# A transformer trunk step in float32 on one core: the first unit and the last output without Strassen sums, start in a written order, pooling rows by pairs

## The chip, the cores and the metric

The kernel runs on one core of a Trainium2 chip. Five engines work side by side, each through its own instructions in order: PE (TensorE, matmuls; its weight loads are shown apart as PEld), DVE (VectorE), ACT (ScalarE), POOL (GpSimd) and SP (SyncE), which here only issues DMAs. PE writes its results to PSUM, eight banks of 128x512 float32 (`banks`); everything else lies in SBUF or, as `dram` tiles, in the chip's memory. The metric is device time of one execution in microseconds (us).

## The reference

One inference step of a hybrid trunk with one layer of each kind, on 512 prompt frames and 8 x 16 sample frames (640 rows in all), in float32. Cut to what matters here:

```python
h = rmsnorm(x, norm_a[l])
z = h @ w_in_a[l]                          # 2048 -> 2 x 4096
u, gate = z[..., :E_A], z[..., E_A:]
y, st = pool_mix(u, pool_prev[l], pos0, w_grp_a[l], scale_a[l])   # trailing means of 2, 4, 8, 16 frames, then a map in each of 4 groups
x = x + (y * jax.nn.silu(gate)) @ w_out_a[l]
new_pool.append(st)                        # last 15 rows of u
...
hk = rmsnorm(x, norm_kv)
kvf = hk @ w_kv
```

After it come keys, values, forget gates, attention over a cache of 256 rows, an output projection and a last norm. All ten outputs are computed.

## The kernel before

**Precision.** Every float32 operand is split in two parts of the faster type float32r: `hi` is a rounded copy made by ACT, `lo` is the rest, a subtraction on DVE. A product is three matmuls: wh x hi, wh x lo, wl x hi. The activations lie transposed: 128 channels by 640 frames, as two halves of 320 (`HALF`).

**Units.** The projection to `u` and the gate is cut into 32 units of 256 output columns; 16 are of kind u, 16 of kind g, in the order u00, u01, g00, u02, g01 and so on. A unit multiplies a 2x2 block of weights with a 2x2 block of activations by Strassen's scheme: seven products m1 to m7 instead of eight, on sums of blocks (`OPER` says which). Eight `Side`s hold the activations, 256 channels each: four blocks, of which three (`bh`, `bl`) serve as they are and four sums of blocks (`th`, `tl`) are made by `blocks_t`. Weights come in slabs of 512 channels (four a unit): `fetch` loads one into `raw` (three buffers), `prep` makes its sums on DVE and splits raw and sums. `pair8` runs a unit, 4 slabs x 7 products x 2 sides x 3 = 168 matmuls, and calls `tick` twice in each slab, by which small jobs (`pool_rows`, `residual`) put an instruction or two into PE's order. `combine` puts the seven products together on DVE.

**Start.** The five row tiles are loaded, normalised (squares on ACT with a running sum, `newton_rsqrt`, scaling on DVE), transposed on PE and copied to the sides. The first unit goes through `first_unit`: all four weight slabs are held at once (the fourth in a pool of its own), and the products on plain blocks run ahead of those on sums.

**A u unit** also transposes 120 old rows (`st`), makes the pooled difference `dd` with shifted additions on POOL (`sw`, one to four of them), stores it, and copies the last 15 rows of each sample stream to `us`. `pool_rows` transposes the two halves of `us` to bank 7 one after the other, with a copy `po` to SBUF and a store on POOL's queue after each.

**Groups.** For each of four groups `y_pair` makes four tiles of y (96 plain matmuls each), times the gate, split as sides 4 to 7; then `out_pair` makes eight pairs of output tiles, 84 Strassen matmuls each, and adds them to the stream in memory (`xacc`) with accumulating DMAs on POOL's queue. In the last group the sum has to be read back: the first part of an output is added in memory, the stream is loaded as `x1` (L589), three more products are added to it on DVE (L605), and the result is stored to `xres`, squared (`squares`, summed by POOL, L640) and split (`split_x`) for the next projections. Tiles 8 to 15 are split after the loop, since their places are in use until then.

**The rest** opens new pools (`wp` for weights, `big`) in the memory that the first part frees, and starts with `prime` and `proj`: weights loaded at L716, scaled by the norm's gain on DVE (L722), split at L730 and L732, multiplied at L701.

**Order.** PE's instructions stand in the order of the program. The other engines' order is made by a scheduler that follows estimated times; a pool's address is set by the order in which pools are opened, and a tile waits for the tiles that held its memory before.

Of the kernel before, what the change touches and what calls it, by code (L numbers as in the profile page):

```python
# [39 lines left out]
def tile_yoco_step(ctx, tc, i, o):  # L40
# [36 lines left out]
    ident = const.tile([P, P], F32, name="ident")  # L77
    make_identity(nc, ident)
    inv = const.tile([P, 16], F32, name="inv")
    for t in range(16):  # L80
        nc.vector.memset(inv[:, t : t + 1], 1.0 / (t + 1))
# [42 lines left out]
    OPER = {"m1": (0, 0), "m6": (5, 5), "m5": (4, 3), "m7": (3, 4), "m2": (2, 2), "m3": (6, 1), "m4": (1, 6)}  # L124
# [12 lines left out]
    xb_, wa, misc = pool(sa, "xb"), pool(sa, "wa"), pool(sa, "misc")  # L137
# [27 lines left out]
    def blocks_t(sd, x4, t, eng=None):  # L165
        eng = eng or nc.vector
        eng.tensor_tensor(t[:, 0, :], x4[:, 0, :], x4[:, 1, :], op=ALU.subtract)
        eng.tensor_tensor(t[:, 1, :], x4[:, 2, :], x4[:, 0, :], op=ALU.add)
        eng.tensor_tensor(t[:, 2, :], x4[:, 2, :], t[:, 0, :], op=ALU.add)
        eng.tensor_tensor(t[:, 3, :], x4[:, 3, :], t[:, 2, :], op=ALU.subtract)  # L170
        sd.th, sd.tl = (tslot(sd.j, q, [P, 4, HALF], F32R) for q in "hl")
        nc.scalar.activation(sd.th, t, AF.Copy)  # L172
        nc.vector.tensor_tensor(sd.tl, t, sd.th.bitcast(F32), op=ALU.subtract)  # L173
# [17 lines left out]
    fourth = []  # L191

    def wbufs(n, shape):

        j = 3 if n == 3 else n % 3 if n < NA else (2, 0, 3, 1)[(n - NA) % 4]
        if j < 3:
            two = [wa.tile(shape, F32R, tag=f"w{q}{j}", name=f"w{q}") for q in "hl"]
            return two, [[t[:, k : k + 1] for k in range(2)] for t in two]
        if n == 3:
            two = [fourth[0].tile(shape, F32R, tag=f"w{q}", name=f"w{q}") for q in "hl"]  # L200
            return two, [[t[:, k : k + 1] for k in range(2)] for t in two]
        return None, [[bslot(k, q, [shape[0], 1] + shape[2:], F32R) for k in range(2)] for q in "hl"]

    def prep():
        n = nprep[0]
        raw = loaded.pop(n).rearrange("p (a b) (s n) -> p a (b s) n", a=2, n=P)
        if loads[n][0] == "s":
# [3 lines left out]
            eng = nc.gpsimd if n >= len(loads) - 16 else nc.vector  # L211
            eng.tensor_tensor(sums[:, :, 2, :], sums[:, :, 1, :], raw[:, :, 1, :], op=ALU.add)
            eng.tensor_tensor(sums[:, :, 3, :], raw[:, :, 3, :], sums[:, :, 2, :], op=ALU.subtract)  # L213
# [56 lines left out]
    cvue = [misc.tile([P, HALF], F32, tag=f"c{q}", name=f"c{q}") for q in "vue"]  # L270
# [26 lines left out]
    for kind, g, p in units:  # L297
        c0 = (E_A if kind == "g" else 0) + g * G_A + p * 2 * P
        for s in range(4):
            loads.append(("s", win[:, 4 * s : 4 * s + 4, c0 : c0 + 2 * P]))  # L300
    for g in range(4):
# [4 lines left out]
        for c in range(8):  # L306
            for s in range(2):
                loads.append(("s", wout[:, g * 8 + 4 * s : g * 8 + 4 * s + 4, c * 2 * P : (c + 1) * 2 * P]))
# [4 lines left out]
    fourth.append(p0)  # L313
# [4 lines left out]
    gains = [bslot(6 + q // 2, "hl"[q % 2], [P, 512]) for q in range(4)]  # L318
    x4s = [tslot(4 + j // 2, "hl"[j % 2], [P, 4, HALF]) for j in range(8)]
    small = pool(start, "small")  # L320

    idle = small.tile([P, P], F32, name="idle")
    nc.vector.memset(idle, 0.0)
    for _ in range(8):
        nc.tensor.matmul(banks[:, 7, :P], idle, idle, start=True, stop=True)
# [4 lines left out]
    def half_rows(t):  # L330
# [4 lines left out]
    half_rows(0)  # L335
    for q in range(4):
        dma(gains[q], i["norm_a"][0][q * 512 : (q + 1) * 512].partition_broadcast(P))
    half_rows(1)
    fetch()
    half_rows(2)  # L340
    half_rows(3)
    half_rows(4)
    for _ in range(2):
        fetch()
    ssq = small.tile([P, TT, 4], F32, name="ssq")
    nbank = [0]
    for t in range(TT):
        ts = slice(t * P, (t + 1) * P)
        n = D // len(rows[t])
        for q in range(4):  # L350
            c = q * 512 % n
            nc.scalar.activation(banks[:, 7, :], rows[t][q * 512 // n][:, c : c + 512], AF.Square, accum_out=ssq[:, t, q : q + 1])
        v = small.tile([P, 1], F32, tag="v", name="v", bufs=2)
        nc.vector.tensor_reduce(v, ssq[:, t, :], axis=AX.X, op=ALU.add)
        nc.vector.tensor_scalar(v, v, 1.0 / D, EPS, op0=ALU.mult, op1=ALU.add)
        rs = small.tile([P, 1], F32, tag="rs", name="rs", bufs=2)
        newton_rsqrt(small, v, rs, [P, 1], "nr")
        for q in range(4):
# [954 lines left out]
```

## Time and profile before

| what | value |
|---|---|
| time, median of 3 runs (lowest, highest) | 2930.67 us (2927.9, 2931.53) |
| the profiled execution | 2930.98 us, span 2929.3 us |
| mean granted clock of PE | 0.981 |
| PE, DVE, ACT, POOL busy | 2794.5, 1935.2, 1027.0, 390.5 us |
| DMA | 390.36 MB, mean 133 GB/s |

The span is from the first to the last instruction. Busy times are unions over an engine's instructions. "Clock" is the share of full clock that PE was granted. A wait is given to what ended it, as far as the semaphores show. A row of the timeline gives start, duration, engine, line, operation, output and input names with their shapes, and in brackets the idle time ahead of it with what ended it. A row of a group gives count, busy time, mean duration in ns, and idle time ahead with what ended it.

```profile
## 2 busy tenths in 40 slices
PE   5899999999999999999986999999999999999998
PEld 4799999989999999999985999999999999999887
DVE  7777877787777848586674755655656666656434
ACT  6333333333334434343332232333333333334222
POOL 1312223133240110202244000000000000000000
PEclk9799999999999999999997999999999999999999
```

Each digit is a fortieth of the span, 73 us. PE falls below nine tenths in the first two and around the twentieth; its clock falls in the second and about the twentieth too.

### The profile page before, as it was taken

To read this page: it belongs to the slowest core of one execution; us is meant where nothing else is said; L and a number is where in the kernel's file an instruction comes from. 1 tells how busy PE (TensorE), PEld (TensorE's weight loads), DVE (VectorE), ACT (ScalarE), POOL (GpSimd) and SP (SyncE) were. 2 spreads that over 40 slices of the span, in tenths; PEclk is the share of its full clock that TensorE was granted. 3 is DMA by queue.
4 is the path that set the end of the run, shared out by engine and by line. 5 is a ranking of instruction groups with operands and counts; after the bars stand their busy time and mean duration, and the time that the engine had idled before them with its cause. 6 is when DMAs were issued, how large, how long until landed. Compare 5 with 4: busy or idle time off the path is not lost.

```text
span 2929.3 us, 46530 instructions
## 1 busy us (share of the span) xinstructions
PE 2794.5 (95%) x18410; PEld 2691.4 (92%) x18410; DVE 1935.2 (66%) x3350; ACT 1027.0 (35%) x1720; POOL 390.5 (13%) x426
## 2 busy tenths in 40 slices
PE   5899999999999999999986999999999999999998
PEld 4799999989999999999985999999999999999887
DVE  7777877787777848586674755655656666656434
ACT  6333333333334434343332232333333333334222
POOL 1312223133240110202244000000000000000000
PEclk9799999999999999999997999999999999999999
DMA  4344443433435786868466644455544455554823
GB/s 136 98 126 130 132 128 121 134 110 115 131 107 182 182 166 171 170 169 171 121 178 175 163 120 118 115 121 124 131 119 115 119 121 119 120 121 105 148 84 111
DMA packets 677643, 390.36 MB, mean 133 GB/s; under 512 B 323920, under 2 KB 632704, under 8 KB 677296
## 3 DMA queue, kind: packets, MB, share of 16 engines
q1 hardware_dynamic: 652256, 320.61, 41.3%
q0 software_dynamic: 25168, 66.78, 10.4%
q8 instruction: 144, 2.36, 0.3%
q14 instruction: 75, 0.61, 0.1%
HBM read 299.34 MB, written 87.95 MB: 132 GB/s over the span
## 4 chain that ended last, share of the span: by engine, by line
PE 42%; DMA 4%; DVE 1%; SPq 1%; POOL 1%; issue 1%; ACT 0%; DVEq 0%; POOLq 0%; ACTq 0%
PE banks L701 30%; PE banks L1205 5%; PE banks L1133 2%; DMA xacc<-m 2%; PE banks L1034 1%; DMA xt<-xres 1%; PE banks L110 1%; SPq L1243 1%; DMA x<-xacc 1%; POOL bh L640 1%; PE banks L1044 0%; PE banks L1045 0%; PE banks L1046 0%; DVE yn L1246 0%; PE banks L1146 0%
## 5 line engine op out<-in xcount | busy, mean ns | idle before, releaser
L246 PE MATMUL banks<-th,wh 128*128 128x320 f32 x1408 | 447.9, 318 | 12.6 <-ACT th L172 12.2
L246 PE MATMUL banks<-tl,wh 128*128 128x320 f32 x1408 | 442.9, 315 | 17.7 <-DVE tl L173 17.7
L246 PE MATMUL banks<-th,wl 128*128 128x320 f32 x1408 | 441.3, 313 | 0.0
L701 PE MATMUL banks<-th,whi 128*128 128x320 f32 x2048 | 399.6, 317 | 22.7 <-ACT whi L730 22.7
L701 PE MATMUL banks<-tl,whi 128*128 128x320 f32 x2048 | 384.0, 309 | 0.0
L246 PE MATMUL banks<-bh,wh 128*128 128x320 f32 x1056 | 332.8, 315 | 14.8 <-DVE x L605 9.8
L701 PEld LDWEIGHTS banks<-th,whi 128*128 128x128 f32 x2048 | 316.1, 189 | 29.0 <-ACT whi L730 23.0
L246 PE MATMUL banks<-bl,wh 128*128 128x320 f32 x1056 | 331.8, 314 | 3.1 <-DVE bl L163 3.1
L246 PE MATMUL banks<-bh,wl 128*128 128x320 f32 x1056 | 331.6, 314 | 0.6 <-DVE wl L89 0.6
L732 DVE TENSOR_TENSOR wlo<-raw,whi 128x512 fp32r<-128x512 f32 x272 | 186.3, 686 | 212.9 <-ACT whi L730 209.9
L701 PEld LDWEIGHTS banks<-tl,whi 128*128 128x128 f32 x2048 | 321.9, 188 | 0.0
L730 ACT ACTIVATE whi<-raw 128x512 fp32r<-128x512 f32 x272 | 171.7, 632 | 398.6 <-PE banks L701 234.3
L89 DVE TENSOR_TENSOR wl<-raw,wh 128x768 fp32r<-128x768 f32 (+1 forms) x200 | 209.4, 1048 | 142.5 <-ACT wh L86 136.3
L86 ACT ACTIVATE wh<-raw 128x768 fp32r<-128x768 f32 (+1 forms) x200 | 173.5, 869 | 342.8 <-issue 156.0
L246 PEld LDWEIGHTS banks<-tl,wh 128*128 128x128 f32 x1408 | 270.4, 192 | 20.9 <-DVE tl L173 20.9
L246 PEld LDWEIGHTS banks<-th,wh 128*128 128x128 f32 x1408 | 270.5, 192 | 17.2 <-ACT th L172 15.2
L246 PEld LDWEIGHTS banks<-th,wl 128*128 128x128 f32 x1408 | 270.0, 192 | 0.0
L89 DVE TENSOR_TENSOR wl<-sums,wh 128x1024 fp32r<-128x1024 f32 x176 | 223.6, 1271 | 42.5 <-ACT wh L86 41.9
L86 ACT ACTIVATE wh<-sums 128x1024 fp32r<-128x1024 f32 x176 | 185.2, 1052 | 188.6 <-DVE sums L213 183.4
L701 PE MATMUL banks<-th,wlo 128*128 128x320 f32 x1024 | 233.7, 309 | 0.2 <-DVE wlo L732 0.2
L701 PE MATMUL banks<-tl,wlo 128*128 128x320 f32 x1024 | 233.7, 309 | 0.0
L246 PEld LDWEIGHTS banks<-bh,wh 128*128 128x128 f32 x1056 | 203.3, 193 | 16.4 <-DVE x L605 10.3
(376 smaller groups left out, 5156.1 us busy)
## 6 DMA issues: line engine op xcount, KB each, us to landing
raw<-in_w_in_a SPq DMA_DIRECT2D x128, 512.0 KB, 4.0
raw<-in_w_out_a SPq DMA_DIRECT2D x64, 512.0 KB, 4.9
raw<-in_w_kv SPq DMA_DIRECT2D x128, 256.0 KB, 3.1
raw<-in_w_in_b SPq DMA_DIRECT2D x128, 256.0 KB, 3.0
raw<-in_w_grp_a SPq DMA_DIRECT2D x32, 512.0 KB, 5.6
kc<-in_cache_k SPq DMA_DIRECT2D x64, 256.0 KB, 4.1
vc<-in_cache_v SPq DMA_DIRECT2D x16, 1024.0 KB, 7.4
raw<-in_w_out_b SPq DMA_DIRECT2D x64, 256.0 KB, 3.2
```

Source lines behind the costliest of these rows:

```text
L86: a = nc.scalar.activation(hi, x, AF.Copy)
L89: nc.vector.tensor_tensor(lo, x, hi.bitcast(F32), op=ALU.subtract)
L110: nc.tensor.transpose(out, x, ident[:n, :n])
L246: nc.tensor.matmul(bank[:, :HALF], w[kk][:, a, :], x, start=first and q == 0, stop=last and q == 2)
L640: nc.gpsimd.tensor_tensor(sqs[0], sqs[0], s, op=ALU.add)
L701: nc.tensor.matmul(acc_[:, s, :HALF], w, x[:, s * HALF : (s + 1) * HALF], start=f, stop=l)
L730: nc.scalar.activation(hi, raw, AF.Copy)
L732: nc.vector.tensor_tensor(lo, raw, hi.bitcast(F32), op=ALU.subtract)
L1034: nc.tensor.matmul(sp[rows, b % 2 * PAST : (b % 2 + 1) * PAST], qs[:, rows], kct[:, b * PAST : (b + 1) * PAST], start=True, stop=True)
L1133: nc.tensor.matmul(po[32 * q : 32 * q + 32, :P], pts[:, j, 32 * q : 32 * q + 32], vc[:, 4 * q + j, :], start=(j == 0), stop=False)
L1205: nc.tensor.matmul(out, (ol if q == 2 else oh)[k][:, ts], wl if q == 1 else wh, start=first and q == 0, stop=last and q == 2)
L1243: dma(xt[at].rearrange("p t (j r) -> p t j r", r=32), xres[n * 512 : (n + 1) * 512].rearrange("(j c) (t a r) -> a c t j r", c=32, a=4, r=3 ...
```

## The change

1. **Start.** DVE, ACT and POOL follow the program's order until the eight sides stand. The sample's rows go first (tile 4, then 0 to 3). The gains are read as one row each and spread over 128 partitions by a matmul with ones into banks 0 to 3. Squares go 1024 columns at a time into SBUF, four idle matmuls (`busy(4)`) follow each tile.
2. **First unit without sums.** Its four slabs are of kind "p" (no sums); `plain_slab` runs all eight block products, 192 matmuls, into banks 0 to 3. The first block of each side gets a split of its own (`b12`). The sums of the sides are made in place (`sums_t`), five on DVE and three on POOL, and split behind the plain slabs' work. The unit's results are copied by ACT instead of `combine`. The fourth weight buffer is gone.
3. **Pooling rows by pairs.** Both halves of `us` lie in one tile, copied by POOL instead of ACT, transposed one after the other into one bank, copied once, stored once, on SP's queue. `st`, `us`, `po` share a ring of two buffers.
4. **Output, first pair of groups 0 to 2** (`c == 0`): all seven products on sides 0 to 2 first, then those on side 3.
5. **Last group.** y is split plain (`yk`), weights are of kind "p", and `last_pair` makes an output pair with 96 plain matmuls. `load_stream_pair` loads the stream's sum ahead of its pair; the result goes back to `xacc` (on SP's queue) and `xres` is gone. The squares' sum is stored by SP.
6. **Pools.** `wa` is opened ahead of `xb`, so that `wp` later lies where the weights were.

The core of the diff:

```diff
-    xb_, wa, misc = pool(sa, "xb"), pool(sa, "wa"), pool(sa, "misc")
+    wa, xb_, misc = pool(sa, "wa"), pool(sa, "xb"), pool(sa, "misc")
...
+    def sums_t(x4, t=None, eng=None):
+
+        eng, t = eng or nc.vector, x4 if t is None else t
+        eng.tensor_tensor(t[:, 1, :], x4[:, 0, :], x4[:, 1, :], op=ALU.subtract)
+        eng.tensor_tensor(t[:, 0, :], x4[:, 2, :], x4[:, 0, :], op=ALU.add)
+        eng.tensor_tensor(t[:, 2, :], x4[:, 2, :], t[:, 1, :], op=ALU.add)
         eng.tensor_tensor(t[:, 3, :], x4[:, 3, :], t[:, 2, :], op=ALU.subtract)
...
-            loads.append(("s", win[:, 4 * s : 4 * s + 4, c0 : c0 + 2 * P]))
+            loads.append(("s" if loads[3:] else "p", win[:, 4 * s : 4 * s + 4, c0 : c0 + 2 * P]))
...
+    steady.enter_context(tc.manual_schedule(engines={mybir.EngineType.DVE, mybir.EngineType.Activation, mybir.EngineType.Pool}))
...
+    def plain_slab(s):
+        wh, wl = parts.pop(0)
+        for j in (2 * s, 2 * s + 1):
+            hi = [b12[j][:, 0, :]] + [xs_[j].hi(q) for q in range(3)]
+            lo = [b12[j][:, 1, :]] + [xs_[j].lo(q) for q in range(3)]
+            for k in range(2):
+                for n in range(2):
+                    for q, (w, x) in enumerate(((wh, hi), (wh, lo), (wl, hi))):
+                        for h in range(2):
+                            nc.tensor.matmul(first[2 * n + h], w[j % 2][:, 2 * k + n, :], x[2 * k + h],
+                                             start=j + k + q == 0, stop=j == 7 and k == 1 and q == 2)
+        done()
...
+    blocks(6)
+    blocks(7)
+    sums(7)
+    sums(0)
+    sums(1)
+    split_t(xs_[0], x4s[0])
+    fetch()
+    prep()
+    split_t(xs_[1], x4s[1])
+    sums(2)
+    plain_slab(3)
...
+        yield
+        tq = tbank()
         for b in range(2):
-            yield
-            tq = tbank()
-            transpose(tq[: NB * PAD, :P], uss[b])
-            po = pu.tile([NB * PAD, P], F32, tag="po", name="po")
-            nc.scalar.activation(po, tq[: NB * PAD, :P], AF.Copy)
-            store2(o["pool_sample"][0].rearrange("b s e -> (b s) e")[:, c0 + b * P : c0 + (b + 1) * P], po)
+            transpose(tq[: NB * PAD, b * P : (b + 1) * P], uss[b])
+        po = pu.tile([NB * PAD, 2 * P], F32, tag="po", name="po", bufs=2)
+        nc.scalar.activation(po, tq[: NB * PAD, : 2 * P], AF.Copy)
+        store(o["pool_sample"][0].rearrange("b s e -> (b s) e")[:, c0 : c0 + 2 * P], po)
...
+        if c == 0:
+
+            for s, kks in ((0, (0, 1)), (1, (0,))):
+                for m in ORDER:
+                    go(m, s, kks)
+            for m in ORDER[:4]:
+                go(m, 1, (1,))
...
+    def last_pair(c, x1, yk):
+        pp = plain(yk)
+        for b in range(2):
+            a = halves(x1[b])
+            for s in range(2):
+                nc.vector.tensor_tensor(a[:, s, :], a[:, s, :], pp[b][s], op=ALU.add)
+            k = 2 * c + b
+            dma(xacc[c][b * P : (b + 1) * P, :], x1[b])
+            squares(k, x1[b])
+            if k < 8:
+                split_x(k, x1[b])
+            else:
+                late.append((k, x1[b]))
```

How it moves instructions is seen at three places. A name with a number is one tile. The first place is DVE ahead of the second unit. Before, `th_159`, `tl_166` and `bh_494` hold blocks of a side and their rounded copies, `x4_498` the sums of such blocks, `tl_504` the low part of a side's sums; `raw`, `sums`, `wh` and `wl` belong to weight slabs:

```order
L163 TENSOR_TENSOR bl_495<-tl_166,bh_494 128x960
L213 TENSOR_TENSOR sums_474<-raw_446,sums_474 128x2x128
L167 TENSOR_TENSOR x4_498<-th_159 128x320
L169 TENSOR_TENSOR x4_498<-th_159,x4_498 128x320
L170 TENSOR_TENSOR x4_498<-th_159,x4_498 128x320
L89 TENSOR_TENSOR wl_479<-sums_474,wh_478 128x2x512
L209 TENSOR_TENSOR sums_714<-raw_484 128x2x256
L173 TENSOR_TENSOR tl_504<-x4_498,th_503 128x1280
L173 TENSOR_TENSOR tl_513<-th_507,th_512 128x1280
```

Now, `th_132` and `tl_133` hold the sums of a side in place, `tl_732` and `tl_736` their low parts, `raw_659` to `wl_744` are the fifth slab, the first of the second unit, and `dd_802` is the pooled difference of the first unit, which needs POOL's `sw_800`:

```order
L84 TENSOR_TENSOR tl_732<-th_132,th_731 128x1280
L84 TENSOR_TENSOR tl_736<-tl_133,th_735 128x1280
L201 TENSOR_TENSOR sums_739<-raw_659 128x2x256
L203 TENSOR_TENSOR sums_739<-sums_739,raw_659 128x2x128
L548 TENSOR_TENSOR dd_802<-sw_800,inv_179 128x1
L550 SCALAR_TENSOR_TENSOR dd_802<-sw_800,ub_783 128x511
L204 TENSOR_TENSOR sums_739<-raw_659,sums_739 128x2x128
L84 TENSOR_TENSOR wl_744<-raw_659,wh_743 128x2x384
```

Before, a slab's sums (`sums_474`) stood between the sides' blocks and sums. Now the sums of the sides come right ahead of the fifth slab, and the rest of that slab (L204, L84) stands behind `dd_802`.

The second place is SP, which issues most DMAs, at the end of the last group. Before, `bh_14915` and `bl_14916` are loads of the stream (`xacc3`), `sqd` is the sum of squares on its way back to SBUF, `raw` from `in_w_kv` the first weights of the next projection, and the rest are inputs of later stages:

```order
L589 DMA bh_14915<-xacc3_90 128x640
L589 DMA bl_14916<-xacc3_90 128x640
L1018 DMA kc_15487<-in_cache_k 32x64x32
L1157 DMA wr_15259<-in_w_kv 128x16x16
L858 DMA bf_15288<-in_b_f 128x16
L873 DMA cl_15303<-in_cache_logf 128x8x16 x2
L780 DMA sq2_15062<-sqd_8802 128x640
L716 DMA raw_15064<-in_w_kv 128x4x128
L716 DMA raw_15066<-in_w_kv 128x4x128
```

Now, `m4_14401` and `x4_14524` are the tiles that hold the stream's finished output, on their way to `xacc3`:

```order
L770 DMA xacc3_68<-m4_14401 128x640 x2
L770 DMA xacc3_68<-x4_14524 128x640
L832 DMA raw_14909<-in_w_kv 128x4x128
L832 DMA raw_14911<-in_w_kv 128x4x128
L770 DMA xacc3_68<-x4_14524 128x640
L796 DMA sqd_8748<-sq_13991 128x640
L832 DMA raw_14913<-in_w_kv 128x4x128
```

Before, the weights stood behind the last loads of the stream, the inputs of later stages and the sum of squares. Now the first two stand ahead of the last store of the stream, and the sum of squares ahead of the third.

The third place is PE in the second unit. `us` are the last rows of the sample's streams from the first unit, which are transposed, `ident` is the identity, the other rows are products of weights (`wh`, `wl`) and a side. Before, the first of the two transposes, and the second 19 rows on:

```order
L246 MATMUL banks_60<-tl_531,wh_752 128x320
L246 MATMUL banks_60<-th_530,wl_753 128x320
L110 MATMUL banks_60<-ident_64,us_784 120x128
L246 MATMUL banks_60<-th_521,wh_752 128x320
L246 MATMUL banks_60<-tl_522,wh_752 128x320
```

```order
L246 MATMUL banks_60<-bl_453,wh_752 128x320
L246 MATMUL banks_60<-bh_452,wl_753 128x320
L110 MATMUL banks_60<-ident_64,us_795 120x128
L246 MATMUL banks_60<-th_521,wh_752 128x320
L246 MATMUL banks_60<-tl_522,wh_752 128x320
```

Now:

```order
L237 MATMUL banks_60<-tl_736,wh_743 128x320
L237 MATMUL banks_60<-th_735,wl_744 128x320
L105 MATMUL banks_60<-ident_172,us_797 120x128 x2
L237 MATMUL banks_60<-th_731,wh_743 128x320
L237 MATMUL banks_60<-tl_732,wh_743 128x320
L237 MATMUL banks_60<-th_731,wl_744 128x320
```

The two transposes stand behind one another, into one bank, with no product between them.

More of the change, by code (lines that the diff above doesn't have):

```diff
@@ new lines, in tile_yoco_step, with busy @@
+    load_rows(2)
+    fetch()
+    load_rows(3)
+    fetch()
+    steady = ExitStack()
+    steady.enter_context(tc.manual_schedule(engines={mybir.EngineType.DVE, mybir.EngineType.Activation, mybir.EngineType.Pool}))
+    ident = const.tile([P, P], F32, name="ident")
+    make_identity(nc, ident)
+    nc.vector.memset(ones, 1.0)
+    nc.vector.memset(idle, 0.0)
+    inv = const.tile([P, 16], F32, name="inv")
+    for t in range(16):
+        nc.vector.memset(inv[:, t : t + 1], 1.0 / (t + 1))
+    def busy(n):
+        for _ in range(n):
+            nc.tensor.matmul(banks[:, 7, :P], idle, idle, start=True, stop=True)
@@ new lines, in tile_yoco_step, with piece, squares @@
+    busy(8)
+    for q in range(4):
+        nc.tensor.matmul(banks[:, q, :], ones, gains[q], start=True, stop=True)
+    tring = Ring([4, 5, 6])
+    def piece(t, q):
+        n = D // len(rows[t])
+        c = q * 512 % n
+        return rows[t][q * 512 // n][:, c : c + 512]
+    def squares(t, h):
+        n = len(rows[t]) // 2
+        for q in range(n * h, n * h + n):
+            r = rows[t][q]
+            nc.scalar.activation(junk[q % 2][:, : r.shape[1]], r, AF.Square, accum_out=ssq[:, t, q : q + 1])
@@ new lines, in tile_yoco_step @@
+    squares(4, 0)
+    squares(4, 1)
+    mean(4)
+    for n, t in enumerate(order):
+        nxt = order[n + 1] if n < 4 else None
+        v, a, rs = (tiny[:, t, q : q + 1] for q in range(3))
+        if nxt is not None:
+            squares(nxt, 0)
+        nc.scalar.activation(a, v, AF.Sqrt)
+        if nxt is not None:
+            squares(nxt, 1)
+        nc.vector.reciprocal(rs, a)
+        nc.vector.scalar_tensor_tensor(a, rs, rs, v, op0=ALU.mult, op1=ALU.mult)
+        nc.vector.tensor_scalar(a, a, -0.5, 1.5, op0=ALU.mult, op1=ALU.add)
+        nc.vector.tensor_tensor(rs, rs, a, op=ALU.mult)
+        copies = []
+        for q in range(4):
+            turn(t, q, copies)
+            for out, b in copies[2 * q - 2 : 2 * q]:
+                nc.scalar.activation(out, b, AF.Copy)
+            if q == 2 and nxt is not None:
+                mean(nxt)
+        busy(4)
+        for out, b in copies[6:]:
+            nc.vector.tensor_copy(out, b)
+        if n in (2, 3):
```

304 lines of the change are left out of this document (150 added, 154 removed).

## The prediction

> **What bounds the kernel now.** I read the busy shares of the page first, then busy time and granted clock by stage, then the list of waits of the matmul engine (PE), and last the rows of single instructions. The stages are cut at matmul starts that the timeline shows: the row loop, first unit, second unit, the other thirty units, and, further down, the outputs of the four groups; the last row here is the gap behind them. A row gives its length, then busy time (and instructions) of PE, its weight loads, DVE, ACT and POOL, then the granted clock, the DMA share and GB/s.
>
> ```profile
> PE 2794.5 (95%) x18410; PEld 2691.4 (92%) x18410; DVE 1935.2 (66%) x3350; ACT 1027.0 (35%) x1720; POOL 390.5 (13%) x426
> ```
> ```profile
> 0.00:45.00 45.00, 21.59 (x97) 19.81 (x97) 32.39 (x98) 32.42 (x84) 0.70 (x6) 1.00 0.61 210
> 45.00:106.30 61.30, 37.93 (x171) 32.74 (x169) 45.15 (x59) 22.88 (x26) 21.34 (x18) 0.75 0.11 31
> 106.30:133.10 26.80, 26.78 (x174) 26.77 (x175) 19.90 (x37) 8.78 (x18) 6.07 (x9) 0.94 0.55 149
> 133.10:910.40 777.30, 755.69 (x5105) 750.99 (x5104) 620.68 (x972) 279.49 (x427) 211.22 (x228) 0.99 0.43 129
> ...
> 1577.50:1600.10 22.60, 0.00 (x0) 0.00 (x0) 10.83 (x15) 5.86 (x9) 10.69 (x24) 0.58 0.79 178
> ```
> ```profile
> 1068.70:1125.00 56.30, 56.27 (x384) 56.24 (x384) 1.00 0.61 150
> ```
>
> PE is the bound nearly everywhere: 95% of the span. One 128x320 matmul costs 56.3 / 384 = 0.1466 us where nothing waits, so time can only come from the places where PE idles or runs at a lower clock, and every added matmul costs 0.147 us. The first 106.3 us hold 47 us of idle PE (23.4 + 23.4); 133 to 910 has 21.6 us; the gap at 1577 is empty. What comes after 1600 the change hardly touches. The waits say who ends the idle time:
>
> ```profile
> PE banks L701 <- ACT whi L730: 22.7, 1, 22.7
> PE banks L110 <- ACT po L485: 21.2, 9, 3.4
> ...
> PE banks L246 <- DVE x L605: 14.1, 4, 5.9
> ```
>
> **Start and first unit.** The profiled run took 2930.98 us, against a median of 2930.67, so I sum against 2931. The row loop ends at 45 with 32.4 us of work on each of DVE and ACT. In the new fixed order a turn is one chain (square root on ACT, four tiny DVE steps, four scalings, transposes, copies), with two squares less and no weight sums in its way, but every engine now waits its turn. I take 1 us gained, the first matmul at about 44, between a loss of 2 and a gain of 6. The gain is behind it: the first unit as eight plain products has 192 matmuls instead of 168 (+24), but needs neither the four block sums nor their splits, which is what PE waits for between 45 and 104. 192 x 0.1466 = 28.1, and with 1.3 us until the first low part (1.15 + 0.48 on DVE) and about 1 us of low clock it ends near 74.5.
>
> What is late next is the second unit, which needs the sums and splits of all eight sides. DVE must do, between 44 and the last split, by these rows and the means of the profile's groups:
>
> ```profile
> L89 DVE TENSOR_TENSOR wl<-sums,wh 128x1024 fp32r<-128x1024 f32 x176 | 223.6, 1271 | 42.5 <-ACT wh L86 41.9
> L89 DVE TENSOR_TENSOR wl<-raw,wh 128x768 fp32r<-128x768 f32 x176 | 180.3, 1025 | 123.6 <-ACT wh L86 117.4 <-PE banks L246 6.1
> ...
> L209 DVE TENSOR_TENSOR sums<-raw 128x512 f32<-128x512 f32 x192 | 148.5, 774 | 7.3 <-DMA raw<-in_w_out_a 3.4 <-DMA raw<-in_w_in_a 0.3
> L213 DVE TENSOR_TENSOR sums<-raw,sums 128x256 f32<-128x256 f32 x176 | 99.7, 566 | 3.6
> L212 DVE TENSOR_TENSOR sums<-sums,raw 128x256 f32<-128x256 f32 x176 | 82.5, 469 | 3.6
> ```
> ```profile
> 46.04 1.15 DVE L163 TENSOR_TENSOR bl<-th,bh 128x960 fp32r<-128x960 f32 x1
> ...
> 64.92 1.49 DVE L173 TENSOR_TENSOR tl<-th 128x1280 fp32r<-128x1280 f32 x1 [3.02 <-ACT th L172]
> 66.33 0.48 DVE L167 TENSOR_TENSOR x<-th 128x320 f32<-128x320 f32 x1
> ```
>
> Eight low parts of 1.15 and eight of 0.48 (13.0); two plain weight slabs of 1.27 (2.5); sums of five sides, 20 x 0.48 (9.6); eight splits of 1.49 (11.9); four weight slabs with sums, each 0.77 + 0.47 + 0.57 + 1.03 + 1.27 = 4.1 (16.4); two more raw parts (2.1); the pooling of the first unit, two tensors of 640 columns (2.6, an estimate by the 0.48 for 320). Sum 58, less about 5 since rows start 0.08 us before the one ahead has ended: 53. So DVE alone is at 97 if it never waits. It waits: for POOL's running sum of the first unit, which sits ahead of the fifth slab's rest in DVE's row (2.5 us), and where ACT stands behind a weight buffer that PE still reads (3 us). And POOL does three sides' sums beside it:
>
> ```profile
> 52.45 0.68 DVE L209 TENSOR_TENSOR sums<-raw 128x512 f32<-128x512 f32 x1
> ...
> 57.55 1.71 POOL L167 TENSOR_TENSOR th<-tl 128x320 f32<-128x320 f32 x1 [56.17 <-DVE x L170]
> ...
> 58.56 1.25 DVE L209 TENSOR_TENSOR sums<-raw 128x512 f32<-128x512 f32 x1
> ```
>
> The same DVE work took 0.68 with POOL still and 1.25 beside POOL's sum, so a POOL sum costs DVE about 0.6; twelve of them cost 7 us, of which I count 4, as the group means hold some. The Trainium skill, page "SBUF — State Buffer", section "SBUF: two separate sides", says that a DVE instruction with two SBUF inputs and a GpSimd one share a port pair as an exclusive lock, held for the whole instruction. The trace agrees that they hold each other up, but 0.6 is a third of POOL's 1.71; what the full hold would give is rival 2. With PE's last 36 matmuls (5.3 us) the second unit ends near 110 instead of 133.1. Gained: 23, between 33 (PE never waits: 74.5 + 0.5 + 24.6 = 99.6) and 10 (DVE gets only the 45.15 / 61.3 = 74% it had in the first unit: 44 + 59 / 0.74 = 123).
>
> **Pooling rows.** Nine times PE stood at the second of two transposes. Why is seen on ACT and POOL at one of them:
>
> ```profile
> 656.40 0.47 PE L110 MATMUL banks<-ident,us 128*120 128x128 f32 x1 [3.45 <-ACT po L485]
> ...
> 656.94 0.47 PE L246 MATMUL banks<-tl,wh 128*128 128x320 f32 x1
> 657.21 0.47 PE L246 MATMUL banks<-th,wl 128*128 128x320 f32 x1
> ```
> ```profile
> 655.13 1.06 ACT L86 ACTIVATE wh<-sums 128x1024 fp32r<-128x1024 f32 x1 [6.77 <-DVE sums L213]
> 656.09 0.26 ACT L485 ACTIVATE po<-banks 120x128 f32<-120x128 f32 x1
> ```
>
> The first copy out of the one bank stood behind a weight split that waited 6.77 us. With both transposes in one bank there is one copy, and the next user of the bank comes some 30 us later; that cover hides even a wait of 7 us. All of 21.2 goes, and about 6 of the lower clock behind the stalls: matmuls start 0.27 us apart behind this one instead of 0.147, for some ten of them, 1.2 us a stall, and not all nine were long enough. New on this path: the copy of `us` moves to POOL and PE needs it 60 matmuls (8.8 us) after a unit ends; it stands ahead of POOL's sums, so I cost it at nothing; were POOL one sum late (up to the 1.71 above, 1.3 on average as an estimate), fifteen units would lose 19. Gained: 27, between 31 (1.2 us for each of the nine) and 8.
>
> **Outputs of groups 0 to 2.** A stage has 672 matmuls, 98.5 us.
>
> ```profile
> 966.70:1068.60 101.90, 99.03 (x674) 98.55 (x673) 70.48 (x116) 44.11 (x72) 19.43 (x19) 1.00 0.80 183
> 1125.00:1231.10 106.10, 102.09 (x674) 101.11 (x673) 72.83 (x119) 45.06 (x72) 19.43 (x19) 0.97 0.80 182
> 1287.40:1389.40 102.00, 99.14 (x674) 98.65 (x673) 70.92 (x117) 44.74 (x72) 19.42 (x19) 1.00 0.81 184
> 1445.70:1577.50 131.80, 110.17 (x674) 107.84 (x672) 79.32 (x113) 46.53 (x67) 60.62 (x63) 0.91 0.56 148
> ```
> ```profile
> 1294.24 1.48 DVE L173 TENSOR_TENSOR tl<-x,th 128x1280 fp32r<-128x1280 f32 x1
> ```
>
> 3.4 + 7.6 + 3.5 = 14.5 us are lost, at the start: side 3's low sums are there 8.2 us in (1295.7 - 1287.5), and PE wants them after 33 matmuls (4.8 us). The new order wants them after 66 (9.7 us). The evacuation of the first four products is then later by as much, against the 1.8 us that the next pair's first product gives it. Gained: 12, between 14.5 and 3.
>
> **Last group's output.** It and the gap behind it take 131.8 + 22.6 = 154.4. Plain it has 768 matmuls (+96), 112.6 us. The sum of the stream is loaded one pair or more ahead, so the waits on L605 go; the low part of the fourth side is ready some 4.4 us in (two scalings of about 0.5 like the additions below, 1.3 on ACT by 1.06 for 1024 columns, 1.49 on DVE), and PE has 36 matmuls (5.3) before it. Behind the last matmul stand, in DVE's row, two additions, a split, a scaling of the first weights, then ACT's split:
>
> ```profile
> 1570.63 0.49 DVE L605 TENSOR_TENSOR x<-x,banks 128x320 f32<-128x320 f32 x1 [11.16 <-DMA x<-xacc]
> ...
> 1576.80 0.82 DVE L89 TENSOR_TENSOR tl<-x,tl 128x640 fp32r<-128x640 f32 x1 [3.11 <-ACT tl L86]
> ...
> 1598.74 0.69 DVE L722 TENSOR_TENSOR raw<-raw,cols 128x512 f32<-128x512 f32 x1 [5.15 <-DMA raw<-in_w_kv]
> 1599.47 0.63 ACT L730 ACTIVATE whi<-raw 128x512 fp32r<-128x512 f32 x1 [9.96 <-DVE raw L722]
> 1600.15 1.43 PE L701 MATMUL banks<-th,whi 128*128 128x320 f32 x4 [22.69 <-ACT whi L730]
> ```
>
> 2 x 0.49 + 0.82 + 0.69 + 0.63 = 3.1, and 0.9 more until the low weights: 4 us in place of 22.7, since the weights' load itself now sits behind a store that is due 5.5 us before the end, in memory that the pair before has freed. The eight late splits run beside PE's first 48 matmuls, and the sum of squares (two POOL adds, a store, a load) is due 11 us in, at the time it arrives. Gained: 154.4 - 112.6 - 4 = 38, between 41 and 27. One more us comes from a warmer clock at the first projection.
>
> **The sum.** 23 + 27 + 12 + 38 + 1 = 101, so 2931 - 101 = **2830**; the bounds, not all at one end at once, make this case 2816 to 2846.
>
> **The rivals.** (1) DVE becomes the bound of the second unit and PE's clock drops as between 45 and 106 (0.75): the first term falls from 23 to 5, 2848. For it: 53 us of DVE work stand for 53 us of PE work; against: only the splits of the last four sides are late. 12%. (2) POOL's sums hold DVE for as long as they run: 12 x 1.71 = 20 us instead of the 4 counted, the second unit ends 16 later, 2846. For it: POOL's row at 57.55; against: 0.6 seen at 58.56. 6%. (3) The pooling stall moves: PE waits for POOL's copy or a late store, 27 becomes 8, 2849. For it: POOL has up to four sums a half in its row; against: the copies stand ahead of them. 10%. (4) The change does not do what it says at the last gap: the first weights or the squares still come late and 15 us stay instead of 4, 2841. 10%. (5) No wait at all in the second unit, the pooling rows and the last output: 2931 - 33 - 31 - 14.5 - 41 = 2812. 8%. (6) Slower: SP's one queue now carries the pooling stores, the stream's stores and their loads between the weight loads, and a store that waits for its data holds the weights behind it.
>
> ```profile
> SPq L187 <- DVE wl L89: 688.1, 132, 26.8
> ```
>
> SP already waits 688 us for weight buffers, since it runs ahead of their use; three split slabs of 42 matmuls (6.2 us each) are 18 us of lead, so it decides only where a store is held longer. To lose the 101 us, each of fifteen pairs of units would have to lose 6.7, a hold of 25 us in every one. 5%, of which 2% just eat the gain. Two of these together, near 2870: 4%. The forecast keeps 45%.
>
> A measurement of this kernel tells about 0.2% (6 us) from no change. Faster by more: 95%; within: 2%; slower: 3%. The range 2812 to 2856 takes in rivals 1 to 5.
>
> **What would show it.** Right: matmuls of the plain unit back to back from about 44 to 74 us; the second unit's end near 110; no idle PE ahead of the `us` transposes; first pairs of groups 0 to 2 without a wait for L173; eight last pairs of 14.1 us each; a gap of about 4 us ahead of the first projection. Wrong: PE in the second unit idle over 15 us with DVE full; a new wait on POOL's copy; SP standing at a store with PE idle at a weight split.

## The result, and the profile after

The changed kernel takes 2863.28 us (median of 4 runs, 2861.51 to 2865.95) against 2929.28 us (4 runs, 2927.01 to 2931.53). The ratio is 0.9775 with a 95% interval of 0.9759 to 0.9792: 66 us faster, where 101 were forecast. The range ended at 2856. The profiled execution has a span of 2861.1 us, 68.2 less than before.

Busy times of the page after the change, in the form of the first row of the prediction:

```profile
PE 2800.3 (98%) x18578; PEld 2698.3 (94%) x18578; DVE 1872.7 (65%) x3253; ACT 996.3 (35%) x1633; POOL 323.6 (11%) x333
```

Next the stages of the changed kernel, cut at the same matmuls as before: row loop, plain first unit, second unit, the other thirty units, y of group 0, outputs of groups 0, 1 and 2, last output with its gap, rest. A row gives its length, then busy time (and instructions) of PE, its weight loads, DVE, ACT and POOL, the granted clock, DMA share and GB/s.

```profile
0.00:42.70 42.70, 29.02 (x145) 20.85 (x145) 25.09 (x81) 27.15 (x66) 0.70 (x6) 1.00 0.54 185
42.70:72.00 29.30, 28.62 (x192) 28.12 (x192) 28.14 (x31) 13.26 (x19) 16.46 (x14) 1.00 0.12 37
72.00:116.40 44.40, 31.83 (x174) 30.14 (x174) 35.34 (x55) 19.95 (x31) 7.71 (x8) 0.81 0.31 90
116.40:889.20 772.80, 758.34 (x5106) 753.70 (x5105) 612.07 (x974) 273.31 (x383) 193.77 (x197) 0.99 0.44 131
889.20:947.20 58.00, 56.62 (x387) 56.39 (x386) 42.05 (x67) 20.53 (x24) 0.73 (x1) 1.00 0.42 134
947.20:1045.70 98.50, 98.50 (x673) 98.50 (x673) 70.39 (x116) 44.43 (x72) 19.38 (x19) 1.00 0.82 189
1102.00:1200.60 98.60, 98.60 (x674) 98.60 (x673) 71.09 (x118) 44.33 (x72) 19.41 (x19) 1.00 0.86 190
1256.90:1355.50 98.60, 98.60 (x675) 98.60 (x674) 70.32 (x116) 42.93 (x68) 18.95 (x19) 1.00 0.84 196
1411.80:1528.10 116.30, 112.81 (x770) 112.54 (x769) 54.89 (x68) 38.14 (x50) 24.34 (x15) 1.00 0.37 126
1528.10:2861.00 1332.90, 1318.47 (x8645) 1231.96 (x8645) 765.87 (x1491) 418.98 (x789) 7.04 (x21) 0.99 0.52 123
```

Set beside the stages before, these rows give the sum by terms (us; the other three y stages, 56.3 each, did not move):

| term | before | after | gained | forecast |
|---|---|---|---|---|
| start to the second unit's end | 133.1 | 116.4 | 16.7 | 23 |
| the other thirty units | 777.3 | 772.8 | 4.5 | 27 |
| y of group 0 | 56.3 | 58.0 | -1.7 | 0 |
| outputs of groups 0 to 2 | 310.0 | 295.7 | 14.3 | 12 |
| last output and gap | 154.4 | 116.3 | 38.1 | 38 |
| rest | 1329.2 | 1332.9 | -3.7 | 1 |

They add up to 68.2. Two terms out of six stand as forecast or a little better. Two thirds of what is missing is in one place: the units, where the pooling rows were to give 27 us. In y of group 0 PE waits 1.4 us for a result of DVE. PE's waits after the change say what stands there now (engine, line waited for, us in total, times, longest):

```profile
PE banks L237 <- ACT cve L275: 10.7, 4, 3.2
...
PE banks L105 <- DMA st<-in_state_pool: 4.5, 1, 4.5
PE banks L237 <- ACT ub L530: 3.9, 1, 3.9
PE banks L817 <- ACT whi L846: 3.5, 1, 3.5
```

The waits on the copy `po` are gone; the first row is new. `cve` is ACT's copy of a unit's first product, the first thing `combine` does, and the next unit's first matmul needs that bank. It is late four times, each time at the end of the gate unit that follows a u unit of group 3. To see where, I take pairs of units (a u and a g unit), from one unit's transposes of `st` to the next but one's: 4 pairs of group 2, then 3 of group 3, before and after. Rows are as above, first of the kernel before, then of the changed one:

```profile
477.80:691.40 213.60, 202.44 (x1364) 201.31 (x1362) 170.43 (x261) 72.68 (x114) 58.05 (x64) 0.98 0.40 121
691.40:852.10 160.70, 153.07 (x1022) 150.49 (x1020) 129.94 (x196) 55.15 (x85) 56.03 (x48) 0.99 0.42 121
```
```profile
465.00:666.20 201.20, 201.00 (x1363) 198.94 (x1362) 167.39 (x261) 71.25 (x103) 52.11 (x56) 1.00 0.43 129
666.20:830.30 164.10, 155.30 (x1022) 153.68 (x1021) 127.53 (x196) 52.86 (x77) 56.19 (x48) 0.97 0.40 118
```

In group 2 a pair went from 53.4 to 50.3 us, with PE idle for 0.2 us in 201. In group 3 it went from 53.6 to 54.7, and PE is as idle as before (8.8 us against 7.6). So the stall is gone in one group and has moved in the other. The 4.5 us of the table are 12.4 gained in group 2, 3.4 lost in group 3, 3.9 lost ahead of group 2 (the pair behind the second unit takes 54.7 us instead of 50.1) and 0.6 lost behind group 3. What is late is seen on DVE in group 3 of the changed kernel (start, duration, engine, line, operation, tiles, and in brackets the idle time ahead and its releaser), with POOL's rows of the same stretch and then ACT's behind it:

```profile
680.29 0.17 DVE L548 TENSOR_TENSOR dd<-sw,inv 128x15 f32<-128x15 f32 x1 [3.25 <-POOL sw L545]
...
683.18 0.42 DVE L204 TENSOR_TENSOR sums<-raw,sums 128x256 f32<-128x256 f32 x1
684.73 2.08 DVE L84 TENSOR_TENSOR wl<-sums,wh 128x1024 fp32r<-128x1024 f32 x1 [1.13 <-ACT wh L81]
686.84 1.84 DVE L201 TENSOR_TENSOR sums<-raw 128x512 f32<-128x512 f32 x1
688.72 1.57 DVE L203 TENSOR_TENSOR sums<-sums,raw 128x256 f32<-128x256 f32 x1
690.33 1.93 DVE L204 TENSOR_TENSOR sums<-raw,sums 128x256 f32<-128x256 f32 x1
```
```profile
684.25 1.47 POOL L545 TENSOR_TENSOR sw<-ub 128x774 f32<-128x774 f32 x1 [1.92 <-DMA dscr<-dd]
685.80 6.17 POOL L545 TENSOR_TENSOR sw<-sw 128x772 f32<-128x772 f32 x3
```
```profile
692.29 1.06 ACT L81 ACTIVATE wh<-sums 128x1024 fp32r<-128x1024 f32 x1 [6.59 <-DVE sums L204]
693.26 0.83 ACT L81 ACTIVATE wh<-raw 128x768 fp32r<-128x768 f32 x1
696.90 1.06 ACT L81 ACTIVATE wh<-sums 128x1024 fp32r<-128x1024 f32 x1 [2.81 <-DVE sums L204]
697.86 0.42 ACT L275 ACTIVATE cve<-banks 128x320 f32<-128x320 f32 x1
```

While POOL makes its four shifted sums (684.3 to 692), the four DVE instructions beside them take 2.08, 1.84, 1.57 and 1.93 us. L204 took 0.42 at 683.18, just ahead of POOL's sums, and L201 and L203 take 0.69 and 0.42 elsewhere in this stretch. DVE also stood 3.25 us at `dd`, which waits for POOL's sums of the first half. ACT's weight split waits 6.59 us for DVE's sums, and the next one 2.81; `cve` stands behind them. This is the theory to test, called **hold** below: POOL's sums keep DVE back, by the hold and by the wait in DVE's row, and the copy `po` before was only the first in ACT's row to be late for it.

### The profile page after: what moved, and what is told of

Read it like the earlier page. It is cut to its first block, busy times and chain, and to the rows that moved or that the text cites. A ratio compares the mean times of both kernels' runs of the same rounds, so it can differ in the third digit from the quotient of the medians.

```text
span 2861.1 us, 46583 instructions
## 1 busy us (share of the span) xinstructions
PE 2800.3 (98%) x18578; PEld 2698.3 (94%) x18578; DVE 1872.7 (65%) x3253; ACT 996.3 (35%) x1633; POOL 323.6 (11%) x333
## 5 line engine op out<-in xcount | busy, mean ns | idle before, releaser
L237 PE MATMUL banks<-th,wh 128*128 128x320 f32 x1280 | 404.9, 316 | 4.6 <-DVE cu L279 2.8
L237 PE MATMUL banks<-th,wl 128*128 128x320 f32 x1280 | 400.2, 313 | 2.8 <-DVE wl L84 2.8
L237 PE MATMUL banks<-tl,wh 128*128 128x320 f32 x1280 | 399.8, 312 | 0.5 <-DVE tl L84 0.5
L237 PE MATMUL banks<-bh,wh 128*128 128x320 f32 x960 | 298.3, 311 | 14.6 <-ACT cve L275 10.7
L237 PE MATMUL banks<-bl,wh 128*128 128x320 f32 x960 | 297.6, 310 | 0.0
L237 PE MATMUL banks<-bh,wl 128*128 128x320 f32 x960 | 297.5, 310 | 0.0
L84 DVE TENSOR_TENSOR wl<-raw,wh 128x768 fp32r<-128x768 f32 (+1 forms) x200 | 209.9, 1051 | 115.9 <-ACT wh L81 115.4
L237 PEld LDWEIGHTS banks<-th,wh 128*128 128x128 f32 x1280 | 244.4, 191 | 8.1 <-DVE cu L279 4.0
L237 PEld LDWEIGHTS banks<-th,wl 128*128 128x128 f32 x1280 | 244.2, 191 | 3.3 <-DVE wl L84 3.3
L237 PEld LDWEIGHTS banks<-tl,wh 128*128 128x128 f32 x1280 | 244.6, 191 | 0.8 <-DVE tl L84 0.8
L84 DVE TENSOR_TENSOR wl<-sums,wh 128x1024 fp32r<-128x1024 f32 x160 | 202.9, 1268 | 48.0 <-ACT wh L81 47.6
L237 PEld LDWEIGHTS banks<-bh,wh 128*128 128x128 f32 x960 | 181.3, 189 | 16.2 <-ACT cve L275 11.8
```

The source lines that it names most:

```text
L84: nc.vector.tensor_tensor(lo, x, hi.bitcast(F32), op=ALU.subtract)
L237: nc.tensor.matmul(bank[:, :HALF], w[kk][:, a, :], x, start=first and q == 0, stop=last and q == 2)
```

## The experiments

Each kernel is the changed one with the edit shown, unless it says otherwise. Times are medians of 4 runs, beside runs of the kernel before on the same chip (2928.5 to 2932.3 us); differences are to 2863.3, which was measured beside 2929.3. The kernel before itself differs by 3.8 us between these sets of runs, so a smaller difference between two experiments says nothing by the times alone.

**1. Pooling rows apart again.**

```diff
-        tq = tbank()
         for b in range(2):
-            transpose(tq[: NB * PAD, b * P : (b + 1) * P], uss[b])
-        po = pu.tile([NB * PAD, 2 * P], F32, tag="po", name="po", bufs=2)
...
+            if b:
+                yield
+            tq = tbank()
+            transpose(tq[: NB * PAD, :P], uss[b])
+            po = pu.tile([NB * PAD, P], F32, tag="pz", name="po")
...
```

> Undone: pooling rows by pairs (two transposes 18 matmuls apart again, each with its own copy and store on POOL's queue; the copy of us stays on POOL). Forecast's reading (the pairs took away 27 us): slower by 24 to 27. Reading of the trace after (the stall is gone in group 2 only, 12 us, and in group 3 it only moved to the copy cve): slower by 10 to 14, with PE waiting for po in groups 2 and 3 and for cve no longer in group 3.

2886.3 us, slower by 23: just under the forecast's 24, and above what I read from the trace after. PE waits for `po` again and for `cve` no more. But what the edit does is not the same in the two groups. Groups 2 and 3:

```profile
467.20:693.00 225.80, 207.44 (x1362) 206.32 (x1361) 168.64 (x261) 70.45 (x106) 56.13 (x64) 0.95 0.39 115
693.00:853.90 160.90, 153.15 (x1023) 150.53 (x1022) 129.04 (x196) 53.78 (x79) 57.83 (x54) 0.99 0.41 121
```

Group 2's pairs take 56.5 us, 3 more than in the kernel before; group 3's take 53.6, 1.1 less than with the pairs of transposes. So beside everything else in the change the edit is worth 25 us in group 2's four pairs and costs 3 in three pairs of group 3. The forecast's size was thus nearly right beside the rest of the change; what it had no term for is that the rest makes these units longer. From the second unit's `st` transposes to group 0's y they take 781.8 us in the kernel before, 799.9 here and 777.4 with the pairs: 18.1 lost (12.2 in group 2, 6.1 in the pair behind the second unit) and 22.5 won back. In group 2 the rows show where it is lost. DVE's pooled difference and ACT's split ahead of `po` at one stall, first of the kernel before, then of this one:

```profile
539.74 0.17 DVE L466 TENSOR_TENSOR dd<-sw,inv 128x7 f32<-128x7 f32 x1 [1.36 <-POOL sw L463]
547.14 1.06 ACT L86 ACTIVATE wh<-sums 128x1024 fp32r<-128x1024 f32 x1 [6.69 <-DVE sums L213]
```
```profile
534.58 0.17 DVE L548 TENSOR_TENSOR dd<-sw,inv 128x7 f32<-128x7 f32 x1 [2.91 <-POOL sw L545]
542.84 1.06 ACT L81 ACTIVATE wh<-sums 128x1024 fp32r<-128x1024 f32 x1 [7.92 <-DVE sums L204]
```

DVE waits longer for POOL, and its last sums of a slab now stand behind a weight split that takes 2.21 us beside POOL's sums; PE waits 4.6 us a stall instead of 2.8. With the pairs ACT's split is as late (7.85 us at 534.69 of the changed kernel), but PE does not feel it: there the cover of 30 us does what the forecast said. Which part of the change put DVE's row in this order was not separated.

**2. Group 3's shifted sums on DVE.**

```diff
-                nc.gpsimd.tensor_tensor(nx[:, e0:], ...
+                (nc.vector if g == 3 else nc.gpsimd).tensor_tensor(nx[:, e0:], ...
```

> Changed: in group 3 DVE makes the four shifted sums of each half, POOL none. Theory hold (POOL's sums keep DVE from its own two-input instructions for as long as they run, and dd waits for POOL in DVE's row): pairs of units in group 3 go from 54.6 to about 50 us, four of them, so faster by 14 to 19, though DVE gets some 7 us a pair more of its own. Rival (DVE has no room in group 3, it is simply its amount of work): pairs get longer, 56 to 60, slower by 6 to 20.

2841.94 us, faster by 21, more than the 14 to 19 expected. Group 3's three pairs:

```profile
668.10:817.30 149.20, 149.20 (x1023) 149.14 (x1022) 129.54 (x220) 54.75 (x76) 9.99 (x24) 1.00 0.44 130
```

PE never idles, 49.7 us a pair. The striking number is DVE's: it has 24 more instructions, and at 0.95 us each (as L545 takes there on DVE) 22.8 us more work, yet its busy time is 129.5 instead of 127.5. The same rows of weight slabs (L84, L201, L203, L204) take DVE 106.9 us with POOL's sums beside them and 89.7 without. So POOL's sums had cost DVE 17.2 us, most of what DVE needs to make them itself.

**3. The sides' sums on DVE.**

```diff
-        sums_t(x4s[j], None, nc.gpsimd if j in (3, 5, 7) else None)
+        sums_t(x4s[j])
```

> Changed: the sums of sides 3, 5 and 7 are made by DVE instead of POOL, 12 x 0.48 = 5.8 us more for DVE. Theory hold (each POOL sum of 1.0 to 2.5 us holds DVE for its whole length, 16.5 us in all): the second unit ends some 5 to 8 us earlier than 116. The forecast's figure (0.6 us of DVE for each): no change within 2 us. Rival (the second unit is bound by DVE's work alone): 4 to 6 us slower.

2853.31 us, faster by 10. DVE in the plain first unit, with POOL's sums beside it (changed kernel), then without:

```profile
53.56 1.83 DVE L158 TENSOR_TENSOR bl<-tl,bh 128x960 fp32r<-128x960 f32 x1
55.32 1.16 DVE L84 TENSOR_TENSOR b<-tl,b 128x320 fp32r<-128x320 f32 x1
```
```profile
54.59 1.15 DVE L158 TENSOR_TENSOR bl<-tl,bh 128x960 fp32r<-128x960 f32 x1
55.66 0.48 DVE L84 TENSOR_TENSOR b<-tl,b 128x320 fp32r<-128x320 f32 x1
```

Each of these takes 0.68 us longer beside POOL, whatever its own length. Eight like these stand between 51.7 and 63.2, and three of sums behind them take 1.05 instead of 0.49: 7.1 us in all. Two ahead of them, at 49.30 and 50.37, stand beside POOL's first sum and take no longer (1.16 and 0.49 us); there it is POOL's sum that is long, 2.53 us. The second unit's `st` transposes, counted from the first plain matmul, come 61.4 us in instead of 69.1 (104.8 less 43.4, and 111.8 less 42.7; 66.2 to 68.1 in the other kernels here that keep these sums on POOL), and the next pair takes 52.1 us instead of 54.7. The scheduler also put the copies of the first unit's results ahead of two splits in ACT's row here, so not all of the 10 us is the hold's; the two were not separated.

**4. `cve` ahead of a weight split.**

```diff
-            advance()
+            if s < 3: advance()
...
-        put("c21", u, "m4", ALU.add)
+        put("c21", u, "m4", ALU.add); advance()
```

> Changed: the slab that was prepared at the start of a unit's last slab is prepared behind combine, so ACT's copy cve stands ahead of its split. Rival order (the stall in group 3 is only cve standing behind a split that waits for DVE): pairs of group 3 go from 54.6 to 50, faster by 14 to 19. Theory hold (DVE itself is late): the wait on cve goes but PE waits for wl or wh instead, pairs of group 3 stay at 54 or more; no change or slower.

2863.52 us, no change. The wait on `cve` stayed (9.8 us, four times; pairs of 53 to 54 us), since the split of the slab ahead of it is late as well (it waits 6.12 us for DVE's sums). One place in the order does not mend a late engine. The experiment speaks against the rival, though less sharply than meant: the wait did not go, it stayed in its place.

**5. The kernel before, with the shifted sums of groups 2 and 3 on DVE**, and nothing else of the change:

```diff
-                nc.gpsimd.tensor_tensor(nx[:, e0:], ...
+                (nc.vector if g >= 2 else nc.gpsimd).tensor_tensor(nx[:, e0:], ...
```

> The kernel before, with one edit: DVE makes the shifted sums of groups 2 and 3, POOL none there. Pooling rows are still apart. Theory hold (the stalls at the second transpose came from DVE being kept back by POOL's sums, and the copy po was only the first to stand behind it): the pairs of units from 528 to 852 us go from 53 to 55 down to 50, faster than before by 22 to 28. Rival (the one bank and its copy make the stall, whoever makes the sums): the waits on po stay at 2 us or more each, faster by 10 at most.

2900.15 us against 2928.53 (ratio 0.9898, 0.9883 to 0.9913): 28 us from one edited line, with pooling rows still apart. Groups 2 and 3, the same pairs as above:

```profile
478.40:677.30 198.90, 198.90 (x1363) 198.79 (x1362) 167.07 (x285) 75.28 (x114) 18.95 (x40) 1.00 0.44 130
677.30:826.40 149.10, 149.10 (x1022) 149.03 (x1020) 129.21 (x220) 56.05 (x85) 11.25 (x24) 1.00 0.44 130
```

No idle PE, and the waits on `po` fall from 21.2 us to 0.5. The one bank and its copy do not make the stall by themselves: with DVE on time PE does not wait for them.

**6. Group 3 without the pooled difference.** The rows are stored from `ub`; `dd` and its wait leave DVE's row, POOL's sums stay.

```diff
+            if g == 3:
+                store2(dscr[4 * g + p][b * P : (b + 1) * P, :], ub[:, PAD : PAD + NT])
+                continue
```

> Left out, in group 3 only: DVE's pooled difference dd (the rows are stored from ub instead, so group 3 of y is computed from other numbers); POOL's sums stay. It takes away DVE's wait for POOL in its row (3.3 us a pair) and 2.5 us of DVE work, and leaves the hold of DVE by POOL's sums (5.9 us a pair). If the hold decides: pairs of group 3 stay at 52 to 54, faster than the changed kernel by 2 to 10. If the wait in DVE's row decides: pairs go to 50, faster by 14 to 19, as with the sums on DVE.

2854.29 us (2850.0 to 2860.4), faster by 9; pairs of 51.3 us, and 2.1 us of waits on `cve` instead of 10.7:

```profile
666.90:820.90 154.00, 151.77 (x1021) 149.05 (x1020) 134.80 (x172) 52.81 (x76) 56.36 (x48) 1.00 0.43 126
```

It falls between the two expectations: of the 5 us that a pair of group 3 loses, 3.4 go with the wait and the 2.5 us of work in DVE's row, and 1.6 stay with the hold alone. Neither is the whole, and the wait and the work were not parted. DVE is busier with 24 instructions fewer (134.8 against 127.5): the rows of weight slabs now take 119.9 us instead of 106.9, more of them beside POOL's sums.

**7. Pools in the old order.**

```diff
-    wa, xb_, misc = pool(sa, "wa"), pool(sa, "xb"), pool(sa, "misc")
+    xb_, wa, misc = pool(sa, "xb"), pool(sa, "wa"), pool(sa, "misc")
```

> Undone: the order of pools alone (xb is opened ahead of wa again), so that the pool of the next weights lies on other memory at the last gap. Forecast's step (the load sits in memory that is freed a pair earlier): without it the gap of 5.5 us ahead of the first projection grows to 10 to 20 us, slower by 5 to 15. Rival (the gap is set by the last stores and splits, not by the memory): within 2 us.

2868.18 us, slower by 5. The wait ahead of the first projection is 9.5 us instead of 3.5 and 2.0, just short of the 10 expected. SP at the last gap, first of the changed kernel, then of this one:

```profile
1518.80 1.19 SPq L832 DMA_DIRECT2D raw<-in_w_kv  x2
1526.08 0.34 SPq L770 DMA_DIRECT2D xacc<-x  x1
```
```profile
1526.73 0.32 SPq L770 DMA_DIRECT2D xacc<-x  x1
1529.17 0.32 SPq L796 DMA_DIRECT2D sqd<-sq  x1
1529.55 1.66 SPq L832 DMA_DIRECT2D raw<-in_w_kv  x3
```

With `wa` first two loads of weights go out 7.3 us ahead of the last store (half a pair), right behind the store at 1518.37, as the forecast said; the order is worth some 5 us, the low end.

**8. First output pair in the old order.** Both `if c == 0` of `out_pair` become `if False`.

> Undone: the order of the first output pair of groups 0 to 2 alone (four products on both halves at once again). Forecast's step (low sums of the last side come 8.2 us into the pair, PE wants them after 4.8 us in the old order and after 9.7 in the new one): the waits come back, three outputs of 102 to 106 us instead of 98.6, slower than the changed kernel by 9 to 15. Rival (the wait goes away anyway since y and the outputs now start later against DVE): within 3 us.

2879.6 us, slower by 16, a little more than expected. The three outputs take 105.1, 105.2 and 103.8 us instead of 98.6: 18.3 in all.

**9. No sums of sides and no shifted sums on POOL** (the edit of 3, and that of 2 for every group; the squares of the last group are still summed there).

> Changed: POOL makes no sums at all; DVE makes those of sides 3, 5 and 7 and all shifted sums of the u units. Theory hold: the gains of both places add, 10 and 21 us, and pairs of group 2 go from 50.2 to 49.7, so 30 to 34 us faster than the changed kernel, 2829 to 2833. Rival (DVE, at 43 of 50 us in group 3 and now with 1 to 3 us more in every unit of the start, has no room there): the second and third units take back 5 us or more, 2836 to 2842.

2828.23 us (2828.01 to 2828.48), ratio to the kernel before 0.9655 (0.9640 to 0.9669): 35 us faster than the changed kernel, a little more than the 10 and 21 of the two edits apart, and the fastest of all. From the third u unit's `st` on every pair is 49.7 or 49.8 us, and the one before it 50.6. DVE's row had room for them.

**10. The same, with the first two loads of `st` on POOL's queue.**

```diff
-        dma(st, ...
+        (store2 if g == 0 and p < 2 else dma)(st, ...
```

> The kernel with no sums on POOL, and the old rows st of the first two u units are loaded through POOL's queue, which is idle there, instead of standing on SP behind weights that wait for a buffer. If the load is what PE waits for at 75 us: its 2.4 us go, faster than without it (2828.2) by 2 to 3. Rival (the splits of the sides are due at the same time, DVE is the bound of the second unit): within 1 us of 2828.

2829.36 us, a ratio to the kernel before of 0.9647 (0.9633 to 0.9662): no gain that these times can tell from none. The traces say more. PE no longer waits for `st` at the first unit's end, and that unit's `st` transposes come at 74.0 instead of 76.1 us. It waits in the second unit for DVE instead, whose `st` transposes come at 105.6 and not at 104.3. Between 73 and 110 us DVE is busy for 35.5 of 37.

## Why the prediction was wrong, step by step

**Pooling rows: the step that failed.** "All of 21.2 goes" held in group 2 and not in group 3. The row that carried it, the copy `po` behind a weight split, had the reason in its brackets (6.77 us, DVE's sums), and I read the split as a thing in the copy's way and not as an engine that was late. With the copy out of the way I asked when that bank is needed next (30 us, right), and not what stands next in ACT's row behind a late DVE: `cve`, whose bank PE needs at once, 10.7 us of waits. The sign that I had set for this term, no idle PE ahead of the `us` transposes, came true all the same: it watched the victim. A second cost was put at nothing: the rest of the change makes these units 18 us longer (experiment 1). Where DVE is not late the term is nearly right. With the edit of experiment 2 the thirty units take

```profile
117.40:871.50 754.10, 751.43 (x5115) 748.95 (x5114) 617.03 (x1010) 275.47 (x383) 132.38 (x165) 1.00 0.45 134
```

754.1 us, by the same cuts: 23 gained where 27 were forecast; the rest is lost in the pair behind the second unit (56.1 us there, 50.1 before). And experiment 5 gives the kernel before 28 without the pairs. Rival 3 had the right sentence, the stall moves, but the wrong place: it was neither POOL's copy of `us` nor a late store. Its time was 2849; the forecast's case of two rivals together, near 2870 at 4%, came nearest.

**Second unit: a term mis-sized.** The plain unit ran from 42.7 to 72, back to back, as forecast (44 to 74.5). The early start is luck: in the six other kernels here with the same start the first plain matmul comes at 44.0 to 46.2. Then the second unit ended at 116.4 and not near 110. The forecast's own terms give 111.8 there (97 for DVE, then 2.5, 3, 4 and 5.3), not 110. And two things were off. Of the 7 us that POOL's sums were to cost DVE I counted 4, since the group means were to hold some; the rows give 7.1 above them. And the first unit's results were copied late, at 80.6, behind splits in ACT's row that waited for DVE (PE waited 3.9 us for them); the forecast had no such term. With the sums on DVE, and those copies ahead, the unit ends at about 109 (experiment 3). Rival 1 (DVE as the bound there, at a lower clock, 5 us left of the term) was partly so: the granted clock of that stretch is 0.81, but 16.7 us of the term stayed.

Rival 2 had full hold, 1.71 us a sum, and the prediction held 0.6 against it as a third of that. But 1.71 was not the sum's own length. In the kernel before, POOL's sum of 57.55 began while this DVE instruction ran, and another sum of the same size ran at 62.70 with DVE idle:

```profile
57.31 1.22 DVE L89 TENSOR_TENSOR wl<-sums,wh 128x1024 fp32r<-128x1024 f32 x1
62.70 0.89 POOL L170 TENSOR_TENSOR th<-tl,th 128x320 f32<-128x320 f32 x1
```

From DVE's end at 58.53 to the sum's end at 59.26 are 0.73 us: as I read it, the rest of the 1.71 was POOL's own wait for DVE (POOL's spans are rough, so this is a reading and no proof). So 0.6 to 0.68 is most of the 0.89 that such a sum takes alone, and as a price it was about right in the start. Beside the shifted sums of 772 columns it is more: L201 takes 1.84 instead of 0.69 and L203 1.57 instead of 0.42, 1.15 more, beside POOL sums of 1.5 to 2.3 us. The rule that the prediction set aside (the Trainium skill, page "SBUF — State Buffer", section "SBUF: two separate sides": one of the two holds the shared ports for its whole instruction and the other is blocked) is thus nearer to these rows than the third of a sum that I made of them. For group 3 I did not apply it at all, though POOL's sums stand there too.

**Outputs of groups 0 to 2: right.** 14.3 against 12, all three stages at the 98.5 us that 672 matmuls cost. Taking the new order out again costs 16.

**Last output and gap: right.** 38.1 against 38; 768 matmuls in 112.8 us as forecast (112.6), then waits of 3.5 and 2.0 us where 4 were expected. What I put on the order of pools is confirmed in kind (experiment 7).

**The clock at the first projection** gave nothing: the rest takes 3.7 us more. That is no effect of the change that I can show: the kernel of experiment 5, whose rest is that of the kernel before, takes 1332.3 us there in its profile (2899.9 less 1567.6), so two kernels with the same rest differ by 3.1 us there.

**Two smaller sums** of the prediction are off without consequence: the bound of 31 for the pooling rows is 32 (21.2 and nine times 1.2), and the parts given for the 4.4 us of the fourth side's low part add up to 3.8.

**Rival 6** (SP's queue): SP did stand at a weight load, and `st` came 4.5 us late at the first unit's end. In the kernel of experiment 10, where it was 2.4 us late, nothing hung on it; in the changed kernel this was not tried.

## What to carry to other kernels

A wait names the instruction that came last, and the row ahead of that instruction says why. If it stood in an in-order queue behind one that was late, follow that one to the engine that is late, before counting the whole wait as gained; taking the named victim out makes the next in the queue the victim. Work moved to an idle engine is not free if that engine keeps a busy one from its own work: compare the same instruction's duration with and without the neighbour, for every place where the two run together.

## What the runs showed of the hardware that was not expected

DVE instructions with two inputs in SBUF and POOL sums seem to take turns here rather than slow each other in proportion: from 51.7 us on the added time, 0.68 us beside POOL sums of 320 columns, does not depend on the DVE instruction's length (0.48 or 1.15 us), and just before, POOL's sum reads 2.53 us while two DVE instructions take no longer than alone. As I read these rows, a POOL row's duration then holds its wait for DVE as well, and is not what the sum costs DVE. Beside sums of 772 columns the added time is larger, 1.15 for L201 and L203, 1.5 for L204 and 0.9 for a weight split (2.08 instead of 1.22), of the 1.5 to 2.3 us that one sum reads. The offload then brings DVE almost nothing: giving 24 sums back to it raised its busy time by 2.0 us in 149, and let PE run without a gap.
